# Multiplying the first gate blocks of a layer norm ahead of the norm, with mean and factor applied at the eviction

## The chip, the cores and the metric

The kernel runs on one core of one Trainium2 chip. The metric is device time in microseconds (us) of one execution; a comparison uses the median of several. Engines: PE is TensorE (matrix products, whose output lies in PSUM), DVE is VectorE, ACT is ScalarE, POOL is GpSimd, SP issues most DMAs. Each engine works through its own list of instructions strictly in the order that the build gave it.

## What is computed

Three layers follow one another on 256 tokens of 1024 features: an even one (gated convolution and gated DeltaNet), an odd one (HGRN2), and an attention block with a feed-forward. The change lies in what closes the first two of them:

```python
x = layer_norm(DEEPNORM_ALPHA * x + s, ln_g[i], ln_b[i])
gate = jax.nn.sigmoid((x @ w_pl_gate[i]).astype(jnp.float32))
x = x + ((p[i] @ w_pl[i]).astype(jnp.float32) * gate).astype(x.dtype)
```

`s` is the layer's output projection, `i` is 0 (even layer) or 1 (odd layer), and `layer_norm` takes mean and variance of each token over its 1024 features.

## The kernel before

**Layout.** Activations lie with features on the 128 partitions and tokens along the free axis: `x` is 8 feature blocks of 128 by 256. Every dense product is exact to float32: weight and input are each split into two float32r parts (high and low), and a 128x128 weight block takes three PE instructions, hi times hi (`xh,hi` or `yh,hi`), hi times the input's low part (`xl,hi`), and low weight times high input (`xh,lo`). A product of one weight block with 256 tokens is thus three instructions.

**Weights.** `Stream` (lines 144 to 167) brings all weights in their order of use, in chunks of 16 blocks (1 MB). `split_chunk` (lines 197 to 213) issues the DMA into `raw` from SP, and for each half of a chunk (8 blocks, 24 PE instructions) lets ACT round `hi<-raw` (L207) and DVE subtract `lo<-raw,hi` (L207, 128x1024). Four buffers each of `hi` and `lo` hold two chunks. A chunk is fetched when the first block of the chunk ahead of it is taken.

**Order.** The order on PE is written out by the program: `products` issues the dense products and calls `side.tick` (class `Side`, lines 102 to 141), which lets side chains put in their small steps when enough products have gone by. The order on the other engines comes from a scheduler at build time. On the chip all of them are fixed lists.

**Closing a layer** (`out_ln_gate`, from line 586; `ln_stats`, `layer_norm`):

1. The output projection ends bank by bank, 24 PE instructions each. When bank j is ready, DVE does `x<-x,psd` (alpha x plus the bank, 128x512, L314), PE transposes these two blocks of x (`psm<-cst,x`, L298), and DVE takes `BATCH_NORM_STATS2` of them (L761).
2. After the last bank DVE aggregates, POOL raises to the power -0.5 (`rs`, L322), DVE forms minus mean times factor (`rs<-mv,rs`), and PE transposes both into a bank `bc` (`psm<-cst,rs`, 4 instructions), so that every partition has the factor and the shift of each token.
3. Meanwhile PE multiplies `p @ w_pl` (48 instructions, `psd<-ph`): exactly one chunk. The `rs` transposes stand 12 instructions before their end.
4. The norm proper: for blocks 0, 1, 2 and 3, 4 and 5, 6 and 7 DVE does `x<-x,psm` twice (times the factor, plus the shift), ACT scales by `ln_g` and adds `ln_b` (`x<-x,prm`), ACT rounds (`yh<-x`) and DVE subtracts (`yl<-x,yh`).
5. The gate's products go in the groups `[[0, 1, 2, 3], [4, 5], [6], [7]]`, with the input block k outside the outputs of a group: 12 PE instructions for each k in the first group. They wait for `yh` and `yl` of block k. The gate's weights are four chunks; the first of them ends 48 instructions into the first group.
6. Evictions: tanh by ACT, then DVE `(th + 1) * pw` and `x + ...`, then the split of x for the next layer. In the odd layer, `fold` prepares x for the attention block, and `rms_stats` has PE transpose the finished blocks of x.

Beside all this the modulation (`mod`) has DVE multiply and sum a 128x1024 tile per step (`wa<-wa,cr`, L960), in the program's order.

The attention block and the feed-forward have had the trick that the change takes over: `folded` (line 1030) multiplies blocks before the rms norm's factor is known, with two more columns (258 instead of 256) for the shift.

Of the kernel before, what the change touches and what calls it, by code (L numbers as in the profile page):

```python
# [14 lines left out]
P = 128  # L15
T = 256
W = T + 2           # with the modulation's shift as further columns
# [7 lines left out]
INVERSE_US = 30.0  # from a group's triangles to their inverses  # L25
# blocks of the modulation beside the even layer's end, the odd layer and the feed-forward, how far apart,
# and how many at a time
MOD = [(13, 4.4, 1), (27, 7.35, 2), (8, 10.0, 2)]
BLK = 16          # 128x128 blocks in one weight chunk


# ------------------------------------------------------------------ host side: layout and constants
def _blocks(w, order):
    """w [K, N] as a run of 128x128 blocks, BLK of them to a chunk: [chunks, 128, BLK * 128]."""
    out = np.empty((len(order) // BLK, P, BLK, P), np.float32)
    for i, (k, m) in enumerate(order):
        out[i // BLK, :, i % BLK] = w[k * P:(k + 1) * P, m * P:(m + 1) * P]
    return out.reshape(len(order) // BLK, P, BLK * P)


def _cols(v):
    """A vector over features as columns: [128, len / 128]."""
# [7 lines left out]
def pairs_order(ms, group, kt):  # L50
    """Feature blocks in groups, k outside the blocks of a group."""
# [6 lines left out]
def out_plan(ks, tail):  # L58
    """Products of an output projection: all eight feature blocks for the first inputs, then the last ones
    bank by bank, so that the banks are ready one after the other."""  # L60
# [5 lines left out]
# order of the even layer's products: GDN heads (q, k, v, z) and blocks of the gated convolution (c, h, z, b)  # L66
EVEN_UNITS = [(u[0], int(u[1])) for u in "h0 h1 h2 h3 c0 h4 c1 h5 c2 h6 c3 h7 c4 c5 c6 c7".split()]
# q and k blocks (fq 0-2, bq 3-5, fk 6-8, bk 9-11), two pairs of heads at a time
QK_BLOCKS = [0, 1, 6, 7, 2, 3, 8, 9, 4, 5, 10, 11]
# order in which the blocks of the mixers' outputs are used  # L70
# [3 lines left out]
GATE_GROUPS = [[0, 1, 2, 3], [4, 5], [6], [7]]  # L74


def consts():
# [16 lines left out]
    lev = []        # rows: left tokens, half 0 where bit l of the row is 0; columns: (head, pair, half)  # L94
# [6 lines left out]
# ------------------------------------------------------------------ device side  # L101
class Side:
    """Chains of small steps, fed into the stream of dense products: a step goes in when the products
    since the last one of its chain have covered its latency."""
# [1342 lines left out]
```

## Time and profile before

| | |
|---|---|
| runs | 1010.33, 1011.32 and 1012.43 us, median 1011.32 us |
| profiled execution, first to last instruction (its span) | 1008.9 us |
| what lies around the span, against the median of the runs | 2.4 us |
| busy share of the span: PE, DVE, ACT, POOL | 97%, 75%, 55%, 5% |
[...]
| norm and gate of the even layer, on the trace | about 317 to 345 us |
| norm and gate of the odd layer, on the trace | about 637 to 676 us |

No time of the profiled execution's own is given apart from its span; the sums below are made against the span and carried over to the median. Times of the trace count from the first instruction. A row of the timeline gives start, duration, engine, line, operation, output<-inputs, and how many instructions it merges; in brackets stands how long the engine had been idle before it and what ended that. PE instructions overlap: one that takes 0.28 us is followed by the next after 0.12 us.

### The profile page before, as it was taken

The page shows a single profiled execution, that of the slowest core. Times are in us where ns is not written, and L with a number is a line of the kernel's source. Part 1 is how long each engine was busy: PE and PEld are TensorE (multiplying, and loading weights), DVE is VectorE, ACT ScalarE, POOL GpSimd, SP SyncE. Part 2 cuts the span into 40 slices and gives each one's busy share as a digit, 9 for nine tenths or more (in the row PEclk, how much of TensorE's full clock was granted, in tenths as well). Part 3 has the DMA queues.
Part 4 walks back from the last instruction along what each step waited for, and adds up shares of the span by engine and source line. Part 5 has one row for each costly group of instructions (what it writes and reads, how often), then busy time and mean ns, then how long its engine had stood idle before and what let it go on. Part 6 is the DMA issues. An engine that isn't in the chain of part 4 may idle for free.

```text
span 1008.9 us, 19096 instructions
## 1 busy us (share of the span) xinstructions
PE 980.0 (97%) x7622; PEld 939.0 (93%) x7622; DVE 760.5 (75%) x1457; ACT 556.2 (55%) x1104; POOL 51.1 (5%) x59
## 2 busy tenths in 40 slices
PE   6999999999999999999999999899999999999998
PEld 5999989999998999998999999898867999999998
DVE  6788777878768978979697996879776787665543
ACT  6765555654644664454555544567556674444431
POOL 1000000000000000000000000000141000000000
PEclk9999999999999999999999999999999999999999
DMA  7445523345556685655556455353523257654560
GB/s 285 154 143 176 167 85 126 129 169 175 217 188 209 230 314 208 214 184 177 193 193 216 173 174 202 126 178 132 192 95 126 105 190 267 220 201 169 184 213 22
DMA packets 34617, 179.58 MB, mean 178 GB/s; under 512 B 7648, under 2 KB 8672, under 8 KB 16608
## 3 DMA queue, kind: packets, MB, share of 16 engines
q1 hardware_dynamic: 34096, 177.77, 50.2%
q8 instruction: 60, 0.98, 0.4%
q10 hardware_dynamic: 432, 0.59, 0.2%
q14 instruction: 29, 0.24, 0.1%
HBM read 177.04 MB, written 1.31 MB: 177 GB/s over the span
## 4 chain that ended last, share of the span: by engine, by line
PE 57%; DVE 7%; issue 4%; ACT 1%; POOL 1%; POOLq 0%; ACTq 0%; DVEq 0%
PE psd L295 49%; PE psm L295 6%; PE psm L298 2%; DVE lo L207 2%; DVE q L305 1%; ACT hi L207 1%; DVE xl L314 1%; DVE mt L314 0%; DVE wa L960 0%; DVE k L305 0%; DVE x L305 0%; DVE at L305 0%; DVE yl L218 0%; POOL hrs L322 0%; DVE lacc L314 0%
## 5 line engine op out<-in xcount | busy, mean ns | idle before, releaser
L207 DVE TENSOR_TENSOR lo<-raw,hi 128x1024 fp32r<-128x1024 f32 x280 | 341.1, 1221 | 131.4 <-ACT hi L207 129.2
L207 ACT CAST hi<-raw 128x1024 fp32r<-128x1024 f32 x280 | 292.9, 1047 | 248.2 <-PE psd L295 235.2
L295 PE MATMUL psd<-xh,hi 128*128 128x256 f32 (+1 forms) x1296 | 375.5, 290 | 0.0
L295 PE MATMUL psd<-xl,hi 128*128 128x256 f32 (+1 forms) x1296 | 366.7, 283 | 0.7 <-DVE xl L314 0.6
L295 PE MATMUL psd<-xh,lo 128*128 128x256 f32 (+1 forms) x1296 | 366.2, 283 | 0.8 <-DVE lo L207 0.8
L295 PEld LDWEIGHTS psd<-xl,hi 128*128 128x128 f32 x1296 | 245.5, 189 | 1.6 <-DVE xl L314 1.1
L295 PEld LDWEIGHTS psd<-xh,lo 128*128 128x128 f32 x1296 | 245.5, 189 | 1.0 <-DVE lo L207 1.0
L295 PEld LDWEIGHTS psd<-xh,hi 128*128 128x128 f32 x1296 | 245.0, 189 | 0.9 <-ACT hi L207 0.2
L295 PE MATMUL psd<-yh,hi 128*128 128x256 f32 x448 | 131.6, 294 | 3.7 <-ACT yh L217 3.7
L295 PE MATMUL psd<-yl,hi 128*128 128x256 f32 x448 | 127.3, 284 | 1.4 <-DVE yl L218 1.3
L295 PE MATMUL psd<-yh,lo 128*128 128x256 f32 x448 | 127.3, 284 | 0.0
L295 PEld LDWEIGHTS psd<-yh,hi 128*128 128x128 f32 x448 | 85.3, 191 | 5.0 <-ACT yh L217 4.3
L295 PEld LDWEIGHTS psd<-yl,hi 128*128 128x128 f32 x448 | 85.4, 191 | 2.5 <-DVE yl L218 2.4
L295 PEld LDWEIGHTS psd<-yh,lo 128*128 128x128 f32 x448 | 84.9, 189 | 0.1
L295 PE MATMUL psd<-hi,xh 128*128 128x512 f32 x144 | 59.1, 410 | 2.3 <-DVE sq L305 2.1
L960 DVE SCALAR_TENSOR_TENSOR wa<-wa,cr 128x1024 f32<-128x1024 f32 x48 | 58.3, 1217 | 1.7 <-ACT cr L317 1.6
L295 PE MATMUL psd<-hi,xl 128*128 128x512 f32 x144 | 56.9, 395 | 0.0
L295 PE MATMUL psd<-lo,xh 128*128 128x512 f32 x144 | 56.9, 395 | 0.0
L295 PE MATMUL psd<-al,hi 128*128 128x256 f32 x176 | 49.8, 283 | 0.0
L295 PE MATMUL psd<-ah,lo 128*128 128x256 f32 x176 | 49.7, 282 | 0.0
L295 PE MATMUL psd<-ah,hi 128*128 128x256 f32 x176 | 49.3, 280 | 0.0
L314 DVE SCALAR_TENSOR_TENSOR t<-psd,prm,t 128x255 f32<-128x255 f32 (+2 forms) x72 | 34.2, 476 | 3.9 <-ACT t L317 3.1
(328 smaller groups left out, 1392.4 us busy)
## 6 DMA issues: line engine op xcount, KB each, us to landing
raw<-in_w_dram SPq DMA_DIRECT2D x140, 1024.0 KB, 4.8
wa<-in_w_ada_dram SPq DMA_DIRECT2D x48, 512.0 KB, 5.0
cr<-in_c_dram SPq DMA_DIRECT2D x3, 512.0 KB, 5.7
out_dram<-fo SPq DMA_DIRECT2D x3, 256.0 KB, 2.1
cst<-in_cst_dram SPq DMA_DIRECT2D x1, 644.0 KB, 8.2
x<-in_xT_dram ACTq DMA_DIRECT2D x2, 256.0 KB, 3.9
x<-in_xT_dram SPq DMA_DIRECT2D x2, 256.0 KB, 4.8
lev<-in_lev_dram SPq DMA_DIRECT2D x1, 508.0 KB, 7.1
```

Of the source, the lines that this page charges most:

```text
L207: i = [nc.scalar.copy(hi, r), nc.vector.tensor_tensor(lo, r, hi.bitcast(F32), ALU.subtract)]
L295: self.nc.tensor.matmul(out, lhsT, rhs, start=start, stop=stop, skip_group_check=True, **k)
L298: self.nc.tensor.transpose(out, in_, self.c("ident")[:in_.shape[0], :in_.shape[0]])
L305: self.nc.vector.tensor_tensor(out, a, b, op)
L314: self.nc.vector.scalar_tensor_tensor(out, a, s, b, op0, op1)
L960: self.tc.keep_in_program_order(nc.vector.scalar_tensor_tensor(w, w, 1.0, c, ALU.mult, ALU.mult, accum_out=self.md(j)[:, i % 8:i % 8 + 1]))
```

## The change

Two of the eight gate blocks are multiplied ahead of the norm.

- When a bank of the output projection is ready, ACT and DVE also write x times `ln_g`, split into high and low, into the tiles `xh` and `xl` (two ACT and two DVE instructions of 128x256 for each of four banks). Two further columns of these tiles hold `ln_g` and `ln_b`.
- After `p @ w_pl`, `folded(2)` multiplies gate blocks 0 and 1 with them: 48 PE instructions of 258 columns, which wait for nothing of the norm. They use up the gate's first chunk of weights.
- At their eviction the two further columns give each output's constants (`lnc`), DVE multiplies by the token's factor and adds the token's shift times the first constant, and tanh takes the second as its bias. For this ACT copies the bank of broadcast factors to a tile `lnb`, after the scaling of the norm's first block.
- The other blocks go in the groups `[[2, 3, 4, 5], [6], [7]]`, from the normed input.
- The build's scratch for dynamic DMAs is cut to 2048, which leaves room for tiles.

```diff
-GATE_GROUPS = [[0, 1, 2, 3], [4, 5], [6], [7]]
+GATE_GROUPS = [[0, 1], [2, 3, 4, 5], [6], [7]]
...
         bs = [self.ps() for _ in range(4)]
         self.banks = 0
+        lg, lb = (self.prm[n][:, i * KT:(i + 1) * KT] for n in ("ln_g", "ln_b"))
+        self.xtiles()
+        gh, gl = self.xs()
+        for c, v in ((T, lg), (T + 1, lb)):
+            self.split(gh[:, :, c], gl[:, :, c], v)
         def ready(j):
             v = x[:, 2 * j:2 * j + 2]
             self.stt(v, v, ALPHA, bs[j].rearrange("p (m t) -> p m t", m=2), ALU.mult, ALU.add)
+            for m in (2 * j, 2 * j + 1):
+                h, l = gh[:, m, :T], gl[:, m, :T]
+                self.act(h, x[:, m], AF.Copy, scale=lg[:, m:m + 1])
+                self.stt(l, x[:, m], lg[:, m:m + 1], h.bitcast(F32), ALU.mult, ALU.subtract)
             self.side.add("ln", self.ln_stats(x, j, st))
...
+        first = self.folded(2)
         if i == 1:
             self.fold_begin(0, 5)
...
         for ms in GATE_GROUPS:
-            bs = [self.ps() for _ in ms[::2]]
-            self.products((xh, xl), [(k, j) for k in range(KT) for j in range(len(ms))],
-                          [(b, c) for b in bs for c in (0, T)], self.normed)
+            if first:
+                self.side.until(lambda: self.normed)
+                bs = [None]
+            else:
+                bs = [self.ps() for _ in ms[::2]]
+                self.products((xh, xl), [(k, j) for k in range(KT) for j in range(len(ms))],
+                              [(b, c) for b in bs for c in (0, T)], self.normed)
...
-                self.act(th, b[:, :n * T].rearrange("p (m t) -> p m t", m=n), AF.Tanh, scale=0.5)
+                if first:
+                    for m, f in enumerate(first):
+                        c = t3([P, 2], "lnc", 2)
+                        nc.vector.tensor_copy(c[:, :1], f[:, T:T + 1])
+                        self.ts(c[:, 1:], f[:, T + 1:W], 0.5)
+                        self.tt(th[:, m], f[:, :T], self.lnb[:, :T])
+                        self.stt(th[:, m], self.lnb[:, T:], c[:, :1], th[:, m], ALU.mult, ALU.add)
+                        self.act(th[:, m], th[:, m], AF.Tanh, scale=0.5, bias=c[:, 1:])
+                    first = None
+                else:
+                    self.act(th, b[:, :n * T].rearrange("p (m t) -> p m t", m=n), AF.Tanh, scale=0.5)
...
+        self.lnb = t3([P, 2 * T], "lnb")
...
             self.normed.update(range(j, j + n))
-            if j:
+            if j == 0:
+                self.act(self.lnb, bc, AF.Copy)
+            else:
                 yield 0.65
...
-    nc = _bacc.Bacc("TRN2", target_bir_lowering=False, num_devices=1)
+    nc = _bacc.Bacc("TRN2", target_bir_lowering=False, num_devices=1, dynamic_dma_scratch_size=2048)
```

The diff does not show what becomes of the fixed lists. Lines of the changed kernel are one or more higher than before (L305 is L306 there). Three places matter.

**DVE, even layer, from the third bank's residual to the norm's factor.** `x_80` is x, `wa` the modulation's step, `rs` the factor. Before:

```order
L314 SCALAR_TENSOR_TENSOR x_80<-x_80,psd_3293 128x512
L207 TENSOR_TENSOR lo_4116<-raw_4113,hi_4115 128x1024
L761 BN_STATS st_3290<-psm_4087 128x6 x2
L314 SCALAR_TENSOR_TENSOR x_80<-x_80,psd_3294 128x512
L207 TENSOR_TENSOR lo_4120<-raw_4113,hi_4119 128x1024
L960 SCALAR_TENSOR_TENSOR wa_4107,modv<-wa_4107,cr_3278 128x1024
L761 BN_STATS st_3290<-psm_4135 128x6 x2
L769 BN_AGGR mv_4142<-st_3290 128x2 x2
```

With the change:

```order
L315 SCALAR_TENSOR_TENSOR x_80<-x_80,psd_3293 128x512
L208 TENSOR_TENSOR lo_4138<-raw_4135,hi_4137 128x1024
L315 SCALAR_TENSOR_TENSOR xl_3296<-x_80,prm,xh_3295 128x256 x2
L788 BN_STATS st_3290<-psm_4105 128x6 x2
L315 SCALAR_TENSOR_TENSOR x_80<-x_80,psd_3294 128x512
L208 TENSOR_TENSOR lo_4142<-raw_4135,hi_4141 128x1024
L315 SCALAR_TENSOR_TENSOR xl_3296<-x_80,prm,xh_3295 128x256 x2
L990 SCALAR_TENSOR_TENSOR wa_4129,modv<-wa_4129,cr_3278 128x1024
L788 BN_STATS st_3290<-psm_4157 128x6 x2
L796 BN_AGGR mv_4164<-st_3290 128x2 x2
```

A pair of `xl` subtractions has come in ahead of each bank's statistics, four pairs in all.

**DVE, even layer, the norm up to the gate's second chunk of weights** (`lo_4229` before, `lo_4251` after). Before:

```order
L305 TENSOR_TENSOR x_80<-x_80,psm_4177 128x256 x4
L305 TENSOR_TENSOR x_80<-x_80,psm_4177 128x512
L218 TENSOR_TENSOR yl_726_4111<-x_80,yh_725_4110 128x256
L305 TENSOR_TENSOR x_80<-x_80,psm_4177 128x512 x2
L218 TENSOR_TENSOR yl_726_4111<-x_80,yh_725_4110 128x256
L305 TENSOR_TENSOR x_80<-x_80,psm_4177 128x512 x3
L218 TENSOR_TENSOR yl_726_4111<-x_80,yh_725_4110 128x512
L960 SCALAR_TENSOR_TENSOR wa_4206,modv<-wa_4206,cr_3278 128x1024
L218 TENSOR_TENSOR yl_726_4111<-x_80,yh_725_4110 128x512
L207 TENSOR_TENSOR lo_4229<-raw_4226,hi_4228 128x1024
```

With the change, after three `x<-x,psm` of 128x256:

```order
L219 TENSOR_TENSOR yl_728_4133<-x_80,yh_727_4132 128x256
L306 TENSOR_TENSOR x_80<-x_80,psm_4199 128x256
L306 TENSOR_TENSOR x_80<-x_80,psm_4199 128x512 x4
L219 TENSOR_TENSOR yl_728_4133<-x_80,yh_727_4132 128x256
L306 TENSOR_TENSOR x_80<-x_80,psm_4199 128x512
L764 COPY lnc_4317<-psd_4246 128x1
L310 TENSOR_SCALAR lnc_4317<-psd_4246 128x1
L306 TENSOR_TENSOR x_80<-x_80,psm_4199 128x512
L219 TENSOR_TENSOR yl_728_4133<-x_80,yh_727_4132 128x512
L990 SCALAR_TENSOR_TENSOR wa_4230,modv<-wa_4230,cr_3278 128x1024
L219 TENSOR_TENSOR yl_728_4133<-x_80,yh_727_4132 128x512
L208 TENSOR_TENSOR lo_4251<-raw_4248,hi_4250 128x1024
```

The chunk's subtraction stands behind the same work as before, plus two small reads of a finished bank. The third `x<-x,psm` has also gained a wait, here with the waits printed:

```order
L306 TENSOR_TENSOR x_80<-x_80,psm_4199 128x256 [waits PE_49]
L306 TENSOR_TENSOR x_80<-x_80,psm_4199 128x256 [waits DVE_49]
L306 TENSOR_TENSOR x_80<-x_80,psm_4199 128x256 [waits Activation_49]
L219 TENSOR_TENSOR yl_728_4133<-x_80,yh_727_4132 128x256 [waits DVE_49,Activation_49]
L306 TENSOR_TENSOR x_80<-x_80,psm_4199 128x256 [waits DVE_49]
```

It is the wait for ACT's copy `lnb` of the same bank, which on ACT stands behind the scaling of block 0; before, the third of the four had no wait.

**DVE, odd layer.** Before, `lo_7703` and `lo_7707` are the gate's second chunk:

```order
L207 TENSOR_TENSOR lo_7703<-raw_7700,hi_7702 128x1024
L314 SCALAR_TENSOR_TENSOR rs_7620<-mv_7619,rs_7620 128x2
L305 TENSOR_TENSOR x_80<-x_80,psm_7662 128x256 x4
L305 TENSOR_TENSOR x_80<-x_80,psm_7662 128x512
L207 TENSOR_TENSOR lo_7707<-raw_7700,hi_7706 128x1024
L218 TENSOR_TENSOR yl_1242_7588<-x_80,yh_1241_7587 128x256 x2
L305 TENSOR_TENSOR x_80<-x_80,psm_7662 128x512 x4
```

With the change, behind all of the norm's `x<-x,psm`, `lo_7755` and `lo_7759` are that chunk:

```order
L219 TENSOR_TENSOR yl_1250_7646<-x_80,yh_1249_7645 128x512
L208 TENSOR_TENSOR lo_7755<-raw_7752,hi_7754 128x1024
L208 TENSOR_TENSOR lo_7759<-raw_7752,hi_7758 128x1024
L219 TENSOR_TENSOR yl_1250_7646<-x_80,yh_1249_7645 128x512 x2
L306 TENSOR_TENSOR xl_7827<-modv,xh_7826 128x8x2
L315 SCALAR_TENSOR_TENSOR q_6982<-lnb_7725,lnc_7830,q_6982 128x256
L764 COPY lnc_7836<-psd_7751 128x1
L310 TENSOR_SCALAR lnc_7836<-psd_7751 128x1
L306 TENSOR_TENSOR q_6982<-psd_7751,lnb_7725 128x256
L208 TENSOR_TENSOR lo_7853<-raw_7850,hi_7852 128x1024
L315 SCALAR_TENSOR_TENSOR q_6982<-lnb_7725,lnc_7836,q_6982 128x256
L208 TENSOR_TENSOR lo_7857<-raw_7850,hi_7856 128x1024
```

Three more rows follow before the first two blocks of x are final: the gate's `q<-q,f` (128x512), one more `lo`, and `x_80<-x_80,q_6982` (128x512). On PE the transposes of these two blocks now stand 36 products into the group `[2, 3, 4, 5]`; before, the first such transposes stood 132 products after the start of the gate, behind the group `[4, 5]`'s first products:

```order
L296 MATMUL psd_7849<-yl_1250_7646,hi_7758 128x256
L296 MATMUL psd_7849<-yh_1249_7645,lo_7759 128x256
L299 MATMUL psm_7896<-cst,x_80 128x128 x4
L296 MATMUL psd_7848<-yh_1249_7645,hi_7758 128x256
L296 MATMUL psd_7848<-yl_1250_7646,hi_7758 128x256
```

What stands behind the transposes on PE cannot pass them.

## Rows read from the trace of the kernel before

**Rows 1.** The page: the span, and busy time of each engine with its share.
```profile
span 1008.9 us, 19096 instructions
PE 980.0 (97%) x7622; PEld 939.0 (93%) x7622; DVE 760.5 (75%) x1457; ACT 556.2 (55%) x1104; POOL 51.1 (5%) x59
```

**Rows 2.** Waits of PE: what it waited for, us in total, times, longest.
```profile
PE psd L295 <- ACT yh L217: 3.7, 3, 2.3
...
PE psm L298 <- POOL rs L322: 1.5, 2, 0.8
```

**Rows 3.** Timeline of PE, norm of the even layer.
```profile
322.82 0.65 PE L298 MATMUL psm<-cst,rs 128*128 128x128 f32 x4 [0.81 <-POOL rs L322]
...
324.61 0.28 PE L295 MATMUL psd<-ph,lo 128*128 128x256 f32 x1
325.87 0.38 PE L295 MATMUL psd<-yh,hi 128*128 128x256 f32 x1 [0.98 <-ACT yh L217]
...
333.93 0.39 PE L295 MATMUL psd<-yh,lo 128*128 128x256 f32 x1
```

**Rows 4.** Timeline of PE, norm of the odd layer.
```profile
642.58 0.65 PE L298 MATMUL psm<-cst,rs 128*128 128x128 f32 x4 [0.72 <-POOL rs L322]
...
643.66 0.28 PE L295 MATMUL psd<-ph,lo 128*128 128x256 f32 x1
646.25 0.39 PE L295 MATMUL psd<-yh,hi 128*128 128x256 f32 x1 [2.31 <-ACT yh L217]
...
654.66 0.28 PE L295 MATMUL psd<-yh,lo 128*128 128x256 f32 x1
```

**Rows 5.** The chain that ended last, one piece: start, us, products.
```profile
665.68 5.75 PE psd L295 x48
```

**Rows 6.** Stretches: length, PE busy, (instructions), granted clock, DMA share, GB/s.
```profile
320.00:330.00 10.00, 7.74 (x57) 1.00 0.45 157
...
643.00:646.00 3.00, 0.94 (x9) 1.00 0.17 71
...
648.00:651.00 3.00, 3.00 (x16) 0.50 0.78 320
```

**Rows 7.** Stretches of DVE: length, busy, (instructions), clock, DMA share, GB/s.
```profile
307.28:321.68 14.40, 12.81 (x25) 1.00 0.67 228
323.51:332.66 9.15, 8.56 (x16) 1.00 0.19 71
...
626.56:640.62 14.06, 12.80 (x24) 1.00 0.47 155
```

**Rows 8.** Timeline of DVE: an `xl` pair and what follows it, odd layer.
```profile
662.76 0.88 DVE L314 SCALAR_TENSOR_TENSOR xl<-x,am,xh 128x256 fp32r<-128x256 f32 x2
663.55 0.69 DVE L314 SCALAR_TENSOR_TENSOR q<-q,f 128x512 f32<-128x512 f32 x1
```

**Rows 9.** Timeline of DVE in both norms: mean and factor, weight subtractions.
```profile
323.51 2.26 DVE L305 TENSOR_TENSOR x<-x,psm 128x256 f32<-128x256 f32 x5 [0.55 <-PE psm L298]
...
332.66 2.35 DVE L207 TENSOR_TENSOR lo<-raw,hi 128x1024 fp32r<-128x1024 f32 x2
...
643.27 2.26 DVE L305 TENSOR_TENSOR x<-x,psm 128x256 f32<-128x256 f32 x5 [0.55 <-PE psm L298]
645.45 1.22 DVE L207 TENSOR_TENSOR lo<-raw,hi 128x1024 fp32r<-128x1024 f32 x1
...
647.25 2.59 DVE L305 TENSOR_TENSOR x<-x,psm 128x512 f32<-128x512 f32 x4
```

**Rows 10.** Groups by shape: line, engine, operation, count | busy us, mean ns.
```profile
L317 ACT ACTIVATE x<-x,prm 128x256 f32<-128x256 f32 x8 | 4.5, 595 | 1.8 <-DVE x L305 1.8
L317 ACT ACTIVATE la<-psd 128x512 f32<-128x512 f32 x6 | 3.6, 596 | 3.8 <-PE psd L295 3.8
...
L1028 DVE COPY shc<-psd 128x1 f32<-128x1 f32 x1 | 0.2, 158 | 0.7 <-PE psd L295 0.7
```

**Rows 11.** The page's DMA issues: tile, count, KB, us from issue to landing.
```profile
wa<-in_w_ada_dram SPq DMA_DIRECT2D x48, 512.0 KB, 5.0
```

## The prediction

> **What bounds the kernel now.** I read the page first: PE is busy 97% of a span of 1008.9 us [rows 1], so only time in which PE stands or runs slowly can be won, and whatever makes PE stand more is lost in full. The table of PE's waits comes next: the largest single wait is for the norm's rounded input `yh` (2.3 us), then POOL's factor `rs`, 1.5 us in two waits [rows 2]. The timeline of PE shows both places. In the even layer the last product of `p @ w_pl` starts at 324.61 and holds PE for 0.12 us; the gate's first product starts at 325.87, its 51st at 333.93 [rows 3]. A product takes 0.12 us (48 in 5.75 us [rows 5]), so 50 of them need 6.0 us of these 9.2: **3.2 us lost**. In the odd layer the same count runs from 643.78 to 654.66 [rows 4]: 10.9 less 6.0, **4.9 us lost**. [...]
>
> What the change can win is thus at most 3.2 + 4.9 = 8.1 us. I then read DVE in the same stretches, since every product also needs its weight chunk's low part from DVE, in a fixed order: from the first bank's residual to the norm's factor DVE is busy 12.81 of 14.40 us in the even layer and 12.80 of 14.06 in the odd one [rows 7]. DVE has little room there, and that is where the change puts its work.
>
> **The change part by part, even layer.**
>
> *Eight `xl` subtractions ahead of the statistics.* A pair holds DVE from 662.76 to 663.55, 0.80 us [rows 8]; four pairs, 3.2 us. The idle time of that stretch is 14.40 - 12.81 = 1.6 us [rows 7]. If it soaks up what it can, the factor comes 3.2 - 1.6 = 1.6 us later. Bounds: 3.2, if none of it does, and 1.2, if a pair holds DVE only 0.7 us; I take 1.6, since the idle time lies in small pieces between the very operations that the pairs join. The `rs` transposes go from 322.82 to 324.4, and PE waits for them 0.8 + 1.6 us, or earlier for a late transpose of x: either way it is 1.6 us behind. The eight ACT scalings beside them (at most 0.6 us each, as `x<-x,prm` [rows 10]) cost nothing: ACT is busy 55% [rows 1], and on DVE a `lo` of 1.2 us stands ahead of each pair and covers the two scalings that it waits for.
>
> *48 folded products ahead of the norm.* They are moved, not added; 2 of 258 columns are new, 96 x 0.12 x 2/256 = 0.1 us for both layers. They start when `w_pl` ends, 324.73 + 1.6 = 326.3, and end 5.8 us later [rows 5] at 332.1. They use up the first gate chunk. The group `[2, 3, 4, 5]` starts on the second one, whose first low half its third product needs at 332.4.
>
> *That low half.* Before, DVE starts it at 332.66, 9.15 us after the norm's first multiplication at 323.51 [rows 7, 9], and PE's 51st product takes it at 333.93 [rows 3]. The order rows show it behind the same work as before. New ahead of it are two small reads (0.16 us alone [rows 10], 0.1 each in a row) and the wait of the third `x<-x,psm` for ACT's copy of the bank: ACT scales block 0 (0.595) and copies 512 columns (0.596, as `la<-psd` [rows 10]), 1.1 us as they overlap. DVE's 0.6 us idle in that stretch [rows 7] can absorb some; I take 0.3. So it starts at 323.5 + 1.6 + 9.15 + 0.2 + 1.1 - 0.3 = 335.3, and with one subtraction (2.35 for two [rows 9]) PE goes on at 336.4. **Before 333.93, after 336.4: +2.5 us** (bounds +1.8, with all 0.6 absorbed and the factor 1.2 us late, and +4.4, with nothing absorbed there or in the tail). PE stands some 4 us at once. The wait of 3.2 us that was to be covered is covered, and a longer one stands in its place.
>
> [...]
>
> *The clock.* A stand of 4 us is longer than the 2.3 us after which the clock fell in the odd layer [rows 4, 6]. I take a fall, **+1.5 us** (bounds 0 and 1.5).
>
> [...]
>
> *Behind it.* DVE's evictions of the first pair (four 128x256 operations of some 0.4, four small ones) stand between later weight halves, each wanted 2.9 us after the last. By the rows above the third half is just in time: 0. If the next `wa` (5.0 us to land [rows 11], where DVE reaches it some 3.6 us after its buffer is free) comes late, up to 0.9 us more.
>
> **Odd layer.**
>
> *Tail.* 3.2 us again, idle 14.06 - 12.80 = 1.3 [rows 7]: factor and first multiplication 1.9 us later, 645.2 instead of 643.27 [rows 9]. PE ends the folded products at 643.78 + 1.9 + 5.8 = 651.5 and wants the second chunk's low half at 651.8.
>
> *That low half* stood early before (645.45, [rows 9]); now it stands behind the norm's multiplications. From 645.2: four 128x256 operations at 0.40 and six 128x512 at 0.65 [rows 9], the wait for ACT 1.1, two `yl` 0.8, one `yl` of 512 columns 0.65, constants 0.2, the first eviction product 0.4: 8.65 us, to 653.85; done at 655.0. PE stands from 651.8 to 655.0, against 654.66 before [rows 4]: +0.35. The whole win of 4.9 us is gone here.
>
> *Then the transposes of x for the next norm.* They stand 36 products into this group on PE and want blocks 0 and 1 of x final. DVE gets there in one busy run from 653.85: two `lo` 2.35, two `yl` 1.3, the small `xl` 0.1, `q` 0.4, constants 0.2, `q` 0.4, `lo` 1.15, `q` 0.4, `lo` 1.15, `q` of 512 columns 0.65, `lo` 1.15, and x 0.7, together 9.95 us: 663.8. PE is there at 655.0 + 34 x 0.12 = 659.1 and waits 4.7 us. Before, the product in this place ran at 654.66 + 34 x 0.12 = 658.7. **Odd layer: 663.8 - 658.7 = +5.1 us** (bounds +4.2, where DVE's small operations overlap better, and +6.4, where no idle time of the tail is used). A slow clock after the first stand lies inside the second wait and costs nothing; one after the second costs 0 to 1.5, and I take **0.7**.
>
> The cut of the DMA scratch I cost at nothing: the page's large queues are issued by SP and ACT, and no load is late in the rows above.
>
> **Sum:** 2.5 + 1.5 + 5.1 + 0.7 + 0.1 = **+9.9 us**, on the span 1018.8, on the median of the runs 1011.3 + 9.9 = **1021 us**. The span lies 2.4 us under the median; I take that difference as unchanged.
>
> **Rivals.**
>
> - *It does what it is meant to do.* The subtractions of the second chunk come in time, as they would if DVE had idle time that the rows don't show, and only the later factor remains: -8.1 + 1.6 + 1.9 + 0.1 = -4.5, 1006.8 us. For it: the folded products depend on nothing of the norm, 5.8 us is longer than each of the waits. Against it: DVE's list is fixed and its idle shares are 1.6 and 1.3 us. It decides by whether DVE begins the second chunk's first low half before 331 us (even) and 650 us (odd), and the x chain ends by 655. Chance 0.04.
> - *Gain and loss cancel*, where the odd layer's x chain is as long as here but the two low halves come in time: -3.2 + 1.6 in the even layer, and the x chain then starts 3 us earlier, +2: 1012 us. Chance 0.03.
> - *The stands come, but the clock stays up in the even layer and after the second stand*, as it did in the even layer before: 1011.3 + 2.5 + 5.1 + 0.1 = 1019.0. Chance 0.25.
> - *DVE's backlog lasts*: the `wa` load comes late (+0.9), the clock falls after all stands (+0.8), and the next layers start with weight splits behind (another 1 to 2): 1024 us and more. Nothing in the stretch after the gate shows such a wait now. Chance 0.10.
>
> My forecast, with the clock falling once more than before or twice, has 0.58.
>
> **How the numbers follow.** Predicted time 1021. The low bounds sum to 1.8 + 0 + 4.2 = +6.0 (1017.3), the high ones to 4.4 + 1.5 + 0.9 + 6.4 + 1.5 = +14.7 (1026); that all high ends come at once belongs to the last rival, and I stop at 1024.2. The range 1017 to 1024.2 leaves out the first two rivals and part of the last, some 0.15. A measurement of this kernel tells about 0.2% (2 us) from no change. Faster 0.04, same 0.03, slower 0.93.
>
> **What would show it.** In the trace of the changed kernel: PE's longest wait in the even norm no longer `yh` from ACT but `lo` from DVE, some 4 us, at the start of the group of four; a PE wait of 4 to 5 us for `x` from DVE (L306) at `psm<-cst,x` in the odd layer's gate, or some 3 us if the clock fell just before; DVE without idle time between `lo_7755` and the final x; the `rs` transposes 1.5 to 2 us later against the output projection's end; granted clock 0.50 in the even layer's gate. I am wrong if PE passes the folded products without a stand of over 2 us in either layer, or if the odd layer's x is final less than 8 us after its second chunk's first subtraction begins.

## The result and the profile after

| | before | changed | predicted |
|---|---|---|---|
| median of the runs, us | 1011.51 (1010.33 to 1012.43, 4 runs) | 1025.57 (1024.42 to 1026.57, 4 runs) | 1021.0 (1017.0 to 1024.2) |
| span of the profiled execution, us | 1008.9 | 1022.6 | 1018.8 |
| mean granted clock | 0.998 | 0.987 | |

The ratio is 1.0139, with a 95% interval of 1.0121 to 1.0157: slower, as predicted, but by 14.1 us instead of 9.9, and outside the range. Of the kernel before, 80 executions were timed in all; 21 of them took 1014.5 us or more, at a mean granted clock of 0.990 to 0.993.

The page of the changed kernel, its head, against [rows 1]:

```profile
span 1022.6 us, 19147 instructions
...
PE 986.8 (96%) x7622; PEld 945.3 (92%) x7622; DVE 770.0 (75%) x1493; ACT 564.8 (55%) x1128; POOL 50.3 (5%) x59
```

PE has the same 7622 records and is busy 6.8 us longer, in a span that is 13.7 us longer: about half of the loss is slower work, the other half standing. Its waits, against [rows 2]:

```profile
PE psd L296 <- DVE lo L208: 8.0, 3, 3.8
...
PE psm L299 <- DVE x L306: 3.2, 2, 2.7
PE psm L299 <- POOL rs L323: 2.6, 2, 1.7
PE psd L296 <- DVE sq L306: 2.1, 1, 2.1
PE psm L299 <- DVE x L315: 1.6, 2, 0.8
```

The waits for `yh` are gone, and 8.0 us for `lo` have come, where the kernel before has 0.8. To find where the time went, the same products of both traces were laid side by side in their order, and the start in the kernel before taken from the start in the changed one. This difference is called the shift; it grows in few places:

| stretch | shift grows by, us | predicted |
|---|---|---|
| before the even norm, where the program is the same | -1.42 | 0 |
| norm and gate of the even layer | +4.63 | 2.5 + 1.5 = 4.0 |
| norm and gate of the odd layer | +4.29 | 5.1 + 0.7 = 5.8 |
| attention block, around 742 us | **+6.19** | 0 |

The first is a small DMA that landed earlier (119.05 instead of 121.69 us), less a fall of the clock at 128.3 us (a granted clock of 0.57 from 128 to 132 us) that the trace of before does not have. Both lie ahead of all that was changed, and the shift up to there differs between the profiles from -2.6 to +1.7 us. The gates lost 8.92 us, near the 9.9 of the sum. The attention block, which the change doesn't touch, lost 6.19.

**The even layer's stand.** The timeline of PE, norm of the even layer (compare [rows 3]):

```profile
323.04 0.65 PE L299 MATMUL psm<-cst,rs 128*128 128x128 f32 x4 [1.66 <-POOL rs L323]
...
324.83 0.28 PE L296 MATMUL psd<-ph,lo 128*128 128x256 f32 x1
...
334.95 0.58 PE L296 MATMUL psd<-yh,lo 128*128 128x256 f32 x1 [3.80 <-DVE lo L208]
```

and DVE in the same stretch:

```profile
325.82 0.42 DVE L306 TENSOR_TENSOR x<-x,psm 128x256 f32<-128x256 f32 x1 [1.21 <-ACT lnb L318]
...
333.68 1.22 DVE L208 TENSOR_TENSOR lo<-raw,hi 128x1024 fp32r<-128x1024 f32 x1
```

PE runs from the last product of `w_pl` straight through the folded ones, then stands 3.80 us for `lo`. The new wait for `lnb` is there, at 1.21 us.

**The odd layer's two waits** on PE (compare [rows 4]):

```profile
657.83 0.58 PE L296 MATMUL psd<-yh,lo 128*128 128x256 f32 x1 [3.43 <-DVE lo L208]
666.12 0.66 PE L299 MATMUL psm<-cst,x 128*128 128x128 f32 x4 [2.67 <-DVE x L306]
```

**The clock.** Three stretches of the changed kernel at a granted clock of 0.50 (columns as in [rows 6], with PEld, DVE, ACT and POOL behind PE):

```profile
333.10:339.90 6.80, 4.95 (x23) 4.96 (x24) 6.80 (x14) 3.14 (x6) 0.00 (x0) 0.50 0.63 216
...
657.40:660.80 3.40, 2.97 (x14) 2.97 (x15) 3.40 (x9) 2.29 (x6) 0.00 (x0) 0.50 0.25 41
742.70:756.40 13.70, 13.70 (x37) 8.62 (x36) 7.52 (x40) 4.61 (x16) 1.18 (x1) 0.50 0.22 78
```

The third is the surprise. The same products in the kernel before, with 0.3 us more at the end, at full clock:

```profile
735.20:743.00 7.80, 7.80 (x38) 5.20 (x37) 7.20 (x39) 4.12 (x15) 1.01 (x1) 1.00 0.40 137
```

PE is busy throughout in both, with 37 and 38 records, for 13.70 us against 7.80: about 6.2 us more for the same products. What PE did just ahead, with the change:

```profile
739.37 0.40 PE L296 MATMUL psd<-lo,xh 128*128 128x512 f32 x1
741.86 0.47 PE L296 MATMUL psd<-hi,xh 128*128 128x512 f32 x1 [2.10 <-DVE sq L306]
...
743.11 1.65 PE L296 MATMUL psm<-kq 64*128 64x128 f32 x4
```

and before:

```profile
734.33 0.47 PE L295 MATMUL psd<-hi,xh 128*128 128x512 f32 x1 [2.11 <-DVE sq L305]
...
735.42 0.92 PE L295 MATMUL psm<-kq 64*128 64x128 f32 x4
```

The stand is an old one and no longer than it was, 2.10 against 2.11 us. Only what followed differs: four `kq` products take 1.65 instead of 0.92 us.

### The profile page after: what moved, and what is told of

Read it like the earlier page. It is cut to its first block, busy times and chain, and to the rows that moved or that the text cites. A ratio compares the mean times of both kernels' runs of the same rounds, so it can differ in the third digit from the quotient of the medians.

```text
span 1022.6 us, 19147 instructions
## 1 busy us (share of the span) xinstructions
PE 986.8 (96%) x7622; PEld 945.3 (92%) x7622; DVE 770.0 (75%) x1493; ACT 564.8 (55%) x1128; POOL 50.3 (5%) x59
## 4 chain that ended last, share of the span: by engine, by line
PE 54%; DVE 7%; issue 4%; ACT 2%; POOL 0%; POOLq 0%; ACTq 0%; DVEq 0%
PE psd L296 46%; PE psm L296 6%; DVE lo L208 2%; PE psm L299 2%; DVE q L306 1%; DVE xl L315 1%; ACT hi L208 1%; DVE wa L990 0%; DVE mt L315 0%; DVE yl L219 0%; DVE k L306 0%; DVE q L315 0%; DVE at L306 0%; ACT x L318 0%; POOL hrs L323 0%
## 5 line engine op out<-in xcount | busy, mean ns | idle before, releaser
L296 PE MATMUL psd<-xh,hi 128*128 128x256 f32 (+1 forms) x1328 | 384.9, 290 | 0.3 <-ACT hi L208 0.3
L296 PE MATMUL psd<-xl,hi 128*128 128x256 f32 (+1 forms) x1328 | 376.0, 283 | 0.8 <-DVE xl L315 0.6
L296 PE MATMUL psd<-xh,lo 128*128 128x256 f32 (+1 forms) x1328 | 375.4, 283 | 0.8 <-DVE lo L208 0.8
L296 PEld LDWEIGHTS psd<-xl,hi 128*128 128x128 f32 x1328 | 251.9, 190 | 1.6 <-DVE xl L315 1.2
L296 PEld LDWEIGHTS psd<-xh,lo 128*128 128x128 f32 x1328 | 251.8, 190 | 1.0 <-DVE lo L208 1.0
L296 PEld LDWEIGHTS psd<-xh,hi 128*128 128x128 f32 x1328 | 251.3, 189 | 1.4 <-ACT hi L208 0.6
L296 PE MATMUL psd<-yh,lo 128*128 128x256 f32 x416 | 119.5, 287 | 7.2 <-DVE lo L208 7.2
L296 PE MATMUL psd<-yh,hi 128*128 128x256 f32 x416 | 123.3, 296 | 0.0
L296 PE MATMUL psd<-yl,hi 128*128 128x256 f32 x416 | 118.4, 285 | 0.5 <-DVE yl L219 0.5
L296 PEld LDWEIGHTS psd<-hi,xh 128*128 128x128 f32 x144 | 27.7, 192 | 10.5 <-issue 4.4
```

The costliest lines, as they stand in the source:

```text
L296: self.nc.tensor.matmul(out, lhsT, rhs, start=start, stop=stop, skip_group_check=True, **k)
```

## The experiments

Two questions: which of the steps in the gates carry the 8.9 us, and why an untouched stretch lost 6.2. "The attention stand" below is the wait of 2.1 us for `sq`, and a kernel or an execution is said to fall when the clock falls behind that stand. Theories on it go by two short names: *place* says that whether the clock falls depends on the moment at which the stand comes, *order* that it depends on where the stand comes behind the fall before it. The expectations also name *content*, that it takes the changed kernel's own work to bring the fall, wherever the stand comes, and *chance*, that some executions of either kernel have it and others not.

This table gives the growth of the shift in one profiled execution of each kernel, worked out as above, and the times. Each ratio is to runs of the kernel before taken beside that kernel, so ratios compare better than medians. The kernels are explained below the table.

| kernel | even | odd | attention | median, us (runs) | ratio to before, 95% |
|---|---|---|---|---|---|
| changed | 4.6 | 4.3 | 6.2 | 1025.57 (4) | 1.0121 to 1.0157 |
| after_again | 3.9 | 6.4 | 6.2 | 1025.81 (5) | 1.0111 to 1.0161 |
| f_lnb | 3.2 | 4.2 | 6.1 | 1024.75 (4) | 1.0079 to 1.0158 |
| f_pool | 3.8 | 3.8 | 6.1 | 1025.10 (4) | 1.0101 to 1.0152 |
| f_xt4 | 3.9 | 2.8 | 4.7 | 1022.91 (4) | 1.0076 to 1.0133 |
| f_all | 0.1 | -1.2 | 6.1 | 1015.82 (10) | 0.9988 to 1.0048 |
| a_fillv | 3.9 | 5.8 | **0.0** | 1019.75 (4) | 1.0068 to 1.0102 |
| f_all_fillv | 0.7 | -1.2 | 0.8 | 1012.02 (10) | 0.9989 to 1.0023 |
| b_fillv | 0 | -0.3 | 0.7 | 1012.36 (10) | 1.0004 to 1.0025 |
| a_even | 3.9 | -0.1 | 6.2 | 1018.12 (10) | 1.0029 to 1.0077 |
| a_odd | 0.0 | 4.3 | 4.7 | 1021.57 (4) | 1.0060 to 1.0112 |
| b_down16 | 0 | 3.3 | 6.2 | 1019.33 (12) | 1.0028 to 1.0076 |

**The changed kernel again.**

> The changed kernel itself, once more, for its executions. Its first four all had the attention stage at half clock (mean clock 0.987 to 0.988, 1024.4 to 1026.6 us). Theory chance: the fall comes in some executions of either kernel and not in others, by where the stand happens to lie; then some 4 in 10 fall (of 39 executions of the kernel before and its two delayed forms 15 had a mean clock of 0.993 or less), and the rest take 1018 to 1021 us at a mean clock of 0.993 or more. Theory content: the changed kernel falls always, and every execution lies at 1024 us or more, clock 0.988 or less.

1025.81 us, and all nine executions of this kernel took 1024.42 us or more. The even layer's 3.9 and the odd layer's 6.4 show how far the two gates vary between executions: in this one the clock fell for 3.4 us in the even layer, not 6.8, and in the odd layer once more, behind the wait for x, at 669.1 us.

**Delays** (b_delay22, b_delay36, a_delay24). The first product of the odd layer's output projection is repeated, which changes no value and only moves what follows.

```diff
+        self.again = 22 * i
...
-            self.mm(o, hi, ph, start=id(b) not in started, stop=False)
+            for _ in range(1 + self.again):
+                self.mm(o, hi, ph, start=id(b) not in started, stop=False)
```

> The kernel before, with the first product of the odd layer's output projection issued 22 times more (it starts a sum, so the repeats change no value); PE and all that follows comes about 1.7 us later (22 x 0.12 = 2.6 less 0.95 of a stand there). The changed kernel ran at half clock for 13.65 us in the attention stage (742.7 to 756.4), behind a stand of 2.10 us that the kernel before has too (2.11), without a fall. Theory place: the stand brings the clock down or not by where in time it lies; moved by 1.7 us it does, and the kernel before takes +1.7 +6 = about +7.7 us, clock 0.5 at some 735 to 750. Theory content: the fall comes from what the change does; then it is +1.7 us, and the clock of the attention stage stays 1.00. Either way a fall behind the odd norm can move by 1.5 us.

> The kernel before, with the same product issued 36 times more: all that follows comes about 3.4 us later. Theory place: not told beforehand which delays bring the fall, but two delays 1.7 us apart should differ: if the one with 1.7 us falls, this one stays at clock 1.00 in the attention stage and takes +3.4 us. Theory content: +3.4 us, clock 1.00, as for every delay. A theory by which every delay of this kernel brings the fall gives +9.5 us.

> The changed kernel, with the same product issued 24 times more: the odd norm and all behind it comes about 1.8 us later. Theory place: the stand in the attention stage is moved out of the bad place and the clock stays up there; the delay makes the kernel FASTER, by 6.2 - 1.8 = 4.4 us against the changed kernel, about +9.7 us against the one before. Theory content: the fall stays, +1.8 us against the changed kernel, +16 us against the one before.

1013.46 (10 runs), 1015.53 (10) and 1029.69 us (4). In their profiles the two delayed forms of the kernel before reached the attention stand 2.7 and 5.2 us later, not 1.7 and 3.4. The kernel before, delayed, kept 1.00 in attention in both profiles, with 3 of 10 executions each about 6 us above the others, much the share that it has undelayed (21 of 80). The changed kernel, delayed, fell for 13.65 us all the same. A delay ahead of the odd gate turns neither kernel into the other: *place* failed here as it was put.

**Filling the attention stand** (a_fill18, a_fillv, b_fillv). Transposes of a tile of ones into free banks, read by no one, stand on PE just ahead of the product that waits for `sq`: 8 in a_fillv, 16 in b_fillv.

```diff
+    def spin(self, n):
+        for q in range(4):
+            b = self.ps("m")
+            for j in range(n):
+                self.tr(b[:, j * P:(j + 1) * P], self.ones)
...
+                if g == 0:
+                    self.spin(2)
```

> The changed kernel, with 18 transposes of a constant (some 2 us of PE work) put on PE just ahead of the product that stands 2.1 us in the attention stage. If the fall of the clock there comes from that stand, it is gone: clock 1.00 from 742 to 756, and about 6 us less than the changed kernel, some +8 us against the one before. If the clock falls for another reason (work of another kind ahead of it, the products of 64 rows behind it), it still falls, and the time stays within 0.5 us of the changed kernel, some +14 us against the one before.

a_fill18 missed its place: its 18 transposes ran at 729.36 us, one group of products too early, and in the profile the stand stayed at 2.1 us and the clock fell behind it. So it does not test the stand. But its four runs are of two kinds: 1027.72 and 1029.65 us (the profiled one) at a mean clock of 0.988 and 0.983, and 1020.12 and 1020.77 us at 0.997 and 0.995, below all nine of the changed kernel. The fall thus seems to stay out in some executions without a fill in the stand itself; why in these is open.

> The changed kernel, with 8 transposes of a constant (0.9 us of PE work in four banks) put right into the stand of 2.1 us of the attention stage, ahead of the products of v; the last fill had stood one group of products too early and left the stand whole. What is left of the stand is some 1.2 us. If this stand brings the clock down there, the 10 to 14 us at half clock in the attention stage are gone in most executions, and the kernel takes some 6 us less, 1018 to 1020 (the sum that was predicted without this fall, 1021, less what the first 120 us vary). If something else brings it (what the gates did before), the fall stays and the time is 1024 to 1027.

> The kernel before with the same 8 transposes in the same place. Of its executions a third lay at 1015 to 1019 us with a mean clock of 0.990 to 0.993. If the stand of the attention stage makes these, they are gone: all of them at 1009.5 to 1013 us, clock 0.995 or more. If not, a third stays above 1015.

The timeline of PE in a_fillv, and the stretch around it:

```profile
742.06 1.04 PE L299 MATMUL psm<-cst,ones 128*128 128x128 f32 x8
744.32 0.47 PE L296 MATMUL psd<-hi,xh 128*128 128x512 f32 x1 [1.23 <-DVE sq L306]
```

```profile
738.00:755.00 17.00, 15.77 (x76) 11.51 (x75) 13.72 (x54) 8.94 (x28) 5.44 (x3) 1.00 0.36 125
```

With 1.04 us of work in it the stand is 1.23 us, the clock stays at 1.00, and the 6.2 us are gone: 1019.75 us, all four runs (1017.86 to 1020.66) below all nine of the changed kernel. That this stand brings the fall in the changed kernel, and that the fall costs 6 us, is shown. Without it the change costs a factor of 1.0085, 8.6 us of the 1010.50 of that set: about the gates' loss.

The same fill in the kernel before, twice as long, gave ten executions between 1009.14 and 1013.10 us, at a cost of 0.14% in the median. That it took the long executions away is likely but not shown: of the 19 of the kernel before beside them only one was long (1017.39), and at 21 of 80 ten without a long one come up by chance in about one case of twenty.

**Mending the gates, one step at a time.** f_lnb moves ACT's copy `lnb` behind the norm's last blocks.

```diff
-            if j == 0:
+            if j == 6:
                 self.act(self.lnb, bc, AF.Copy)
-            else:
+            if j:
```

> The changed kernel, with ACT's copy of the factors' bank moved behind the norm's last multiplication alone. The prediction costs the wait of DVE for this copy at 1.1 us in each layer. If that is right, DVE's third multiplication starts 1.2 us earlier in both layers and the stand at the second chunk shrinks from 3.8 to some 2.7 us and from 3.4 to some 2.2; in the odd layer the wait for x takes part of it back; 1 to 3 us less than the changed kernel at the same clock in the attention stage. If DVE makes the time up anyway, the stands stay as long, 0 us.

DVE no longer waits there:

```profile
325.96 2.26 DVE L306 TENSOR_TENSOR x<-x,psm 128x256 f32<-128x256 f32 x5 [0.55 <-PE psm L299]
```

In the even layer PE's stand for `lo` is 3.1 instead of 3.8 us. In the odd layer that stand falls from 3.4 to 1.6 us, and the wait for x, which one busy run of DVE ends, grows from 2.7 to 4.4. Less the shift that each trace has ahead of the odd layer, PE takes x at 661.5 us, where the changed kernel takes it at 662.9: the wait for the copy was worth 1.4 us there. The profile shows no win all the same (4.2 against 4.3), because the clock fell behind the longer wait and stayed at 0.50 from 665.1 to 668.4 us. The four runs differ too: three took 1024.41 to 1025.42 us, and one 1016.61 at a mean clock of 0.997, so with this edit the fall in the attention block can stay out.

f_pool gives the second chunk's two subtractions to POOL, f_xt4 puts the transposes of x later on PE in the odd layer, and f_all has these two and f_lnb's edit.

```diff
-            i = [nc.scalar.copy(hi, r), nc.vector.tensor_tensor(lo, r, hi.bitcast(F32), ALU.subtract)]
+            i = [nc.scalar.copy(hi, r), (nc.gpsimd if late == 2 and h in (0, 1) else nc.vector).tensor_tensor(lo, r, hi.bitcast(F32), ALU.subtract)]
...
-            self.w.late = j == 3
+            self.w.late = 2 * (j == 3)
...
-        yield 1.9 if o == self.slots - 1 else 3.0
+        yield 1.9 if o == self.slots - 1 else 3.0 + 4.0 * (o == 0 and self.slots == 5)
```

> The changed kernel, with the two low halves of the gate's second chunk subtracted by POOL in place of DVE, in both layers. If DVE's full list is what makes PE stand at that chunk (the prediction's step), the stands of 3.8 and 3.4 us are gone or under 1 us, and with them the half clock behind them (2.2 and some 0.9 us); the wait for x in the odd layer stays, and some DVE work slides back to the odd layer's start: 3 to 6 us less than the changed kernel at the same clock in the attention stage. Rival: the chunk is late for another reason (its load, ACT's rounding) or POOL is as late (if 128x1024 takes it over 4 us): the stands stay, 0 us or a loss.

> The changed kernel, with the first transposes of the odd layer's finished x held back by products worth 4 us more (some 32 products later on PE). By the prediction's step on these transposes the wait of 2.7 us for x (the second stand of the odd layer) goes, and nothing replaces it: 2.7 to 4 us less than the changed kernel in executions with the same clock. Rival: x is late for its own reason and the wait comes back at the later place, under 1 us gained.

> The changed kernel with three repairs: the second chunk's low halves on POOL, ACT's copy of the factors' bank behind the norm's last multiplication (so that DVE does not wait for it), and the odd layer's first transposes of x held back by 4 us. If the prediction's three steps are the whole loss in both gates, no stand of over 2 us is left there, the clock stays at 1.00 in both, and the kernel takes 3 us less than the one before at the same clock in the attention stage (its 8.1 us of stands won, less some 1.6 and 1.9 for the later factor and 1.4 for DVE work slid back), some 12 less than the changed one. Rival: another part of the change (the 258-column products, the evictions on DVE) costs as much, and it stays 3 us or more above the one before.

f_xt4 took the wait of 2.7 us away (0.5 is left) and won 1.5 us in the odd gate, 4.3 to 2.8, with the clock down there for 6.8 us instead of 3.4. f_pool cut the stands for `lo` to 1.8 us at most but won little: the odd layer's wait for x grew to 4.4, and 2.05 of the even layer's 3.8 us came only at the start of the odd layer, to which DVE's work had slid. DVE's own operations also took longer beside POOL's subtraction: a `yl` of 128x256 took 2.10 us in the odd layer, where the changed kernel has 0.42 (more in the last section). None of the three alone brings the gates back, and all three together do (pairs were not run): f_all has no wait for `lo` over 1.5 us, +0.1 in the even layer and -1.2 in the odd one, where 3 us of win were expected for both. Its attention stand is the old one (2.1 us), and its ten executions lie in two heaps, six from 1014.59 to 1018.39 us and four from 1010.35 to 1011.88. The latter lie where most executions of the kernel before beside them do (ten of 15 at 1009.51 to 1011.94).

**Both mended** (f_all_fillv: f_all with the fill, 16 transposes).

> The changed kernel with its three repairs (POOL, copy, transposes) and the 8 transposes in the stand of the attention stage. If the two losses are independent, it has neither the stands in the gates nor the fall in the attention stage: 1008 to 1011 us in nearly all executions, the same as or 1 to 2 us below the kernel before with the same transposes. If the repairs only moved the loss, it stays 3 us or more above that.

1012.02 us, ten executions from 1010.11 to 1013.49: the same as the kernel before (1010.50 in that set), within its interval, and 0.3 us from b_fillv with the same fill (1012.36). The largest of the ten lies below the six long ones of f_all, so the fill works here too. That is the best version of the change that was found, and it beats nothing. Where the win of the folded products goes, f_all's waits of PE from 300 to 700 us show:

```profile
PE psd L296 <- DVE lo L208: 2.8, 2, 1.5
PE psm L299 <- POOL rs L323: 2.8, 2, 1.7
...
PE psm L299 <- DVE x L315: 1.6, 2, 0.8
```

The kernel before has 3.7 us for `yh` and 1.5 for `rs` there [rows 2]. The waits for `yh` are gone, but PE still waits for DVE's later work: for `lo`, for the later factor, and for a bank's residual x ahead of its statistics.

**When the clock falls behind the attention stand.** One half of the change each (a_even, a_odd: the folded products and the new groups in one layer alone), and delays behind the odd layer's own fall (b_down16: the kernel before, with the first product of gate block 7 run 16 more times; a_down28: the changed one, with that of block 6 run 28 more times).

```diff
-GATE_GROUPS = [[0, 1], [2, 3, 4, 5], [6], [7]]
+GATE_GROUPS = [[[0, 1], [2, 3, 4, 5], [6], [7]], [[0, 1, 2, 3], [4, 5], [6], [7]]]
+AHEAD = 0
...
-        first = self.folded(2)
+        first = self.folded(2) if i == AHEAD else None
```

```diff
+            self.again = 16 * (i == 1 and ms == [7])
```

> The change in the even layer alone, the odd layer as before. By the prediction +2.5 +1.5; in the changed kernel's trace the shift grew by 4.8 there. Theory order: the odd layer's fall is the one of the kernel before, so a quarter to a third of the executions falls in the attention stage; most executions at 1013 to 1016 us, a few at 1020 to 1023. If the even layer's falls decide, nearly all fall: 1020 to 1023.

> The change in the odd layer alone, the even layer as before. By the prediction's steps +5.1 +0.7 in the odd layer; in the changed kernel's trace the shift grew by 4.2 there. Theory order: the last fall ahead of the attention stage is that of the odd layer's gate, the same as in the changed kernel, so the clock falls in the attention stage in nearly all executions: 1020 to 1023 us. If the even layer's falls have a part in it, a third to a half of the executions stays at 1014 to 1016.

> The kernel before, with the first product of the odd layer's last gate group issued 16 times more: the attention stage comes about 1.5 us later, behind the odd layer's own fall of the clock (the earlier delays stood ahead of it and changed nothing of how often the clock fell in the attention stage: 3 of 10 and 3 of 10 executions, as 14 of 57 of the kernel before). Theory order: each fall of the clock puts the work behind it into a new place, and only what lies between the last fall and the stand counts; then this delay, behind the last fall, turns the third of executions that fall into nearly all: 1017 to 1020 us in most. Theory content (only the changed kernel's own work makes it fall always): a quarter to a third falls as before, the rest 1011 to 1014.

> The changed kernel, with the first product of the odd layer's gate group of block 6 issued 28 times more: the attention stage comes about 1.8 us later, behind the odd layer's last fall. Theory order: the stand of 2.1 us then lies where it lay in the kernel before, and in most executions the clock no longer falls there: 1019 to 1022 us, less than the changed kernel although it does more (+1.8 - 6.2). Theory content: all fall, 1026 to 1029 us.

b_down16 is the clearest: nothing of the change is in it, and 9 of its 12 executions took 1017.51 us or more and the other three at most 1013.57, where 21 of 80 without the delay took 1014.5 or more. The delay was meant as 1.5 us; in the profile the odd layer lost 3.3, with the clock down there for 6.8 us, which began ahead of the repeats. Its attention block is the changed kernel's:

```profile
738.82 0.54 PE L298 MATMUL psd<-hi,xh 128*128 128x512 f32 x1 [2.10 <-DVE sq L308]
```

```profile
739.00:752.70 13.70, 13.70 (x36) 8.54 (x36) 7.46 (x39) 3.45 (x15) 1.73 (x2) 0.50 0.23 78
```

A later start of the same stand, brought about behind the odd layer's fall, thus goes with a common fall, which the delays ahead of it (b_delay22, b_delay36) did not bring. That speaks for *order*, but the two runs that were to turn it round did not: a_down28, at 1026.72 us (4 runs), still fell in its profile, for 10.24 us, and a_even, with only the even layer changed, fell, by the times, in 7 of 10 executions (1018.00 us or more; the other three 1013.02 to 1014.26), where a third at most was expected. a_odd fell in its profile (10.24 us, +4.7) and its four runs lie between 1019.24 and 1022.20 us.

So each half of the change makes this fall likelier, and so did one of three delays in the kernel before; what decides it in a single execution stays open.

## Why the prediction was off

**What held.** The account of the two gates, step by step. All times below are taken with the shift that the trace already had at that place (-1.42 us in the even layer, 3.21 in the odd one).

- *The tail of the statistics*: the `rs` transposes were to come 1.6 us later, at 324.4 less 1.4, and came at 323.04.
- *The second chunk's low half, even layer*: to start at 333.9, and started at 333.68; PE to go on at 335.0, and went on at 334.95, after a stand of "some 4 us" that measured 3.80. The term of +2.5 came out at 334.95 - 333.93 + 1.42 = 2.4. The wait for `lnb`, 1.1 by the ACT rows, measured 1.21 and 1.43.
- *The odd layer's chain on DVE*: x was to be final at 663.8 + 3.2 = 667.0, and PE took it at 666.12. DVE began its run with the first subtraction at 656.55, 0.5 us ahead of the forecast, and the run was 9.5 us long, not 9.95, so the +5.1 measured +4.2, its lower bound. With the clock down ahead of it, the wait was 2.67, as "some 3 us" had it.
- *That the change's own aim is met and lost*: PE passes the norm without a wait for `yh`, and a longer one for `lo` stands in its place. f_all shows the other side: with DVE unburdened at these steps, the two gates together lose nothing (+0.1 and -1.2 us).

**What failed is the step "The clock"**, in its list of places. It asked what the new stands would do to the clock, and took +1.5 in the even layer and +0.7 in the odd one. The old stand of 2.1 us for `sq` in the attention block was in the trace of before, about as long as the 2.3 us behind which the clock fell in the odd layer [rows 4, 6], and kept 1.00 in that execution. The prediction never listed it, though the table of waits that it read has it:

```profile
PE psm L295 <- ACT xh L217: 4.5, 1, 4.5
PE psd L295 <- ACT yh L217: 3.7, 3, 2.3
PE psd L295 <- DVE sq L305: 2.1, 1, 2.1
```

The prediction called 2.3 us for `yh` the largest single wait and went on to `rs`. The largest is 4.5 us for `xh`, at the program's start, and the line on `sq` stands between `yh` and `rs`. Its sum thus puts the attention block at nothing, without a reason. With the change the clock fell there in both profiles and, by the times, in all nine executions. That cost 6.2 us, which a_fillv took away again. The longer quarter of the executions of the kernel before may be those that paid for this stand; none of them was profiled. Had the clock of the changed kernel stayed up in the attention block, its time would have been about 1020 us by that run (1019.75), within the range.

The same step was off by less in two more ways. The even layer's fall lasted 6.8 us and not the 3 of [rows 6], so it cost 4.63 - 2.44 = 2.2 instead of 1.5. The 1.5 is half of the 3.00 us at 0.50 in [rows 6]; in that fall of the kernel before, 15 products from 648.04 to 651.24 us follow one another after 0.213 us instead of 0.12, a loss of 1.4. In the odd layer the clock fell behind the first stand alone, where the wait for x takes the loss in, and not behind that wait, so the 0.7 was 0. These two cancel, and the chain's 0.9 is most of what is left between 8.92 measured in the gates and 9.9. That the two falls cancel is luck of this execution: in after_again, where they lay otherwise, the gates lost 3.9 and 6.4.

In the changed kernel's profile the falls at 333.1 and 657.4 us begin within the stands of 3.80 and 3.43 us, and the one at 742.7 begins 0.8 us behind the end of the stand of 2.10. What ends a fall was not shown: from 742.70 on PE's record of work has no gap (13.70 us of 13.70), and the granted clock stayed at 0.50 for all of it; the rows count the engine as busy, with small products, of 64 rows, among them.

**The range** ended at 1024.2, where the last rival began ("DVE's backlog lasts"). That rival had the right size and the wrong mechanism: DVE waited for no `wa` load, so that its term (0.9, where 5.0 less 3.6 would be 1.4) was 0, and no backlog of DVE reached the attention block.

## What to carry to other kernels

A change that moves the work behind it in time also moves every old stand there: list all stands of PE nearly as long as one behind which the clock has fallen anywhere in the trace (here 2.1 and 2.3 us), price each with what runs behind it (here 10 to 14 us at half clock), and put that into the range even where the change touches nothing. A fill of 1 us of harmless work in such a stand is a cheap test, and here worth 6 us. And look at the idle time of the engine that a trick burdens: here DVE had 1.3 to 1.6 us ahead of the wait and was given 3.2 us more, and only the name of what was late changed.

## What the hardware showed beside

**A slower `yl` beside POOL's subtraction.** In f_all_fillv two of the weights' subtractions run on POOL:

```profile
328.53 4.96 POOL L208 TENSOR_TENSOR lo<-raw,hi 128x1024 fp32r<-128x1024 f32 x2 [4.61 <-ACT hi L208]
```

DVE in the same stretch:

```profile
327.04 0.42 DVE L219 TENSOR_TENSOR yl<-x,yh 128x256 fp32r<-128x256 f32 x1
327.39 1.27 DVE L306 TENSOR_TENSOR x<-x,psm 128x512 f32<-128x512 f32 x2
328.79 2.43 DVE L219 TENSOR_TENSOR yl<-x,yh 128x256 fp32r<-128x256 f32 x1
331.15 1.99 DVE L306 TENSOR_TENSOR x<-x,psm 128x512 f32<-128x512 f32 x3
```

The same `yl` takes 0.42 us ahead of POOL's work and 2.43 within it, ending at 331.2, just behind POOL's first subtraction (328.53 and half of 4.96, 331.0). The three `x<-x,psm` of 128x512 behind it keep their 0.66 us each (1.99 in all) while POOL's second one runs. In the odd layer of the same run two `yl` of 128x256 take 2.42 and 1.79 us beside POOL's two subtractions of 2.40 and 2.39. Why `yl` takes longer and `x<-x,psm` does not was not shown.

**One stand, two outcomes.** The same wait of 2.1 us for `sq` was followed by a granted clock of 1.00 in the profiles of the kernel before, b_delay22 and b_delay36, and by 10 to 14 us at 0.50 in those of the changed kernel, b_down16 and f_all. A single profile does not tell what a stand of that length costs.
